# The last projection of a SwiGLU MLP by seven half-size products, with its weight sums made in DRAM

## The chip, the cores and the metric

One core of a Trainium2 chip runs the program. The metric is the time of one execution on the device in microseconds (us), as the median of several executions; lower is better. The engines of the core are TensorE (PE in the profile), VectorE (DVE), ScalarE (ACT), GpSimd (POOL) and SyncE (SP), and 16 DMA engines that all queues share.

## The reference

Two sequences, of 512 and 1024 tokens with 1024 features, go through one layer; everything is float32. With 128 tokens to a tile that is 12 tiles.

```python
D_MODEL = 1024
D_FF = 2816                                     # -(-8 * D_MODEL // (3 * 256)) * 256
def swiglu(hn, w_gate, w_up, w_down):
    return (jax.nn.silu(hn @ w_gate) * (hn @ w_up)) @ w_down
def trunk(x, ...):
    x = x + hybrid_mixer(rmsnorm(x, norm1_g), w_in, ..., w_out)   # dilated attention and gated linear attention
    x = x + swiglu(rmsnorm(x, norm2_g), w_gate, w_up, w_down)
    return rmsnorm(x, final_norm_g)
```

`w_gate` and `w_up` are 1024 x 2816, `w_down` is 2816 x 1024.

## The kernel before

A matrix product in float32 is made of three matmuls of a reduced form: each operand is split into a high part (rounded on ScalarE, L70) and a low part (the remainder, on VectorE, L71), and high x high, high x low and low x high are added in PSUM (`mm3`, L84 to L86). The operations of one engine run in the order in which its queue holds them; a scheduler sets that order from the program's order and the dependencies, and each instruction waits at the head of its queue until its inputs are there.

**The mixer**, 0 to about 920 us, is a list `steps` of some 500 small functions that one loop calls in order: norms of the input rows (`x_a`, `x_b`; their rows come from DRAM by SP's queue at L147), projections, gated linear attention (`Gla`: `e3k_ag` and `e3k_bg` at L607 are multiplied on POOL, the `kv` matmuls at L643 read them), attention, and the output projection. Names that end in `a` or `ag` belong to the first sequence, those in `b` or `bg` to the second. POOL has little to do: among it one power per norm, `rs_n1b` (`rms_rstd`, L65), which VectorE takes to scale the row (L154) before TensorE turns it. Weights and rows come by DMAs on SP's queue, in its order.

**The MLP**, from about 920 us on, works on two blocks of six token tiles; the three pairs of tiles (`NP`) give 3 x 128 = 384 columns (`H`) to each row half. The 2816 features are cut into 11 groups of 256, that is, two halves of 128. Gate and up projections are already made by seven products of half-size matrices (Winograd's form of Strassen's algorithm): `product(wn, n)` is 12 matmuls of 128x384 (L1075) on one combination of weight quarters (`Weights.prepare`, sums on VectorE at L1036, then the split) and one combination of inputs (`b.B[x]`, made once per block by `Block.turn` and kept in DRAM). `common` (L1080) adds the products on VectorE, `w_gate` applies the silu, `w_up` multiplies (L1121) and splits the result into `g`.

The last projection is made in the plain way: `down(i)` (L1129) takes tile i, and for each of two column halves of 512 makes 6 matmuls of 128x512 (two feature halves by three) into a PSUM tile `dn`, which VectorE adds to the running sum `acc` (the tiles `xa`, L1142). The order is a list of units: seven gate products of a group, then the six `down` of the group before, then seven up products. One group thus has 168 gate and up matmuls and 72 down matmuls.

Weights come by `raw` (L1023): 1 MB per group and matrix, `rw_gate`, `rw_up` and `rd` (for `w_down`), each fetched when the one before is used up.

Of the kernel before, what the change touches and what calls it, by code (L numbers as in the profile page):

```python
# [43 lines left out]
def tile_trunk(ctx: ExitStack, tc: tile.TileContext, a: dict):  # L44
# [7 lines left out]
    FORMS = ("b11", "t2", "b21", "t3", "t1", "t4", "b22")  # L52
    formd = {x: [dram.tile([P, 4, 384], F32, name=f"{x}{w}_d") for w in "hl"] for x in FORMS}

# [53 lines left out]
    if True:  # L108
# [758 lines left out]
        for f in steps:  # L867
            f()
        right.close()
# [4 lines left out]
    if True:  # L874
# [5 lines left out]
        g2 = cf.tile([P, D], F32, name="g2")  # L880
# [8 lines left out]
        class Block:  # L889
# [35 lines left out]
            def turn(self, q, tr_p, tag):  # L925
# [21 lines left out]
                sub = lambda o, i0, i1: nc.vector.tensor_tensor(out=o, in0=i0, in1=i1, op=ALU.subtract)  # L947

# [4 lines left out]
                def b11():  # L953
                    tr = quarter(0, 0)
                    sub(t[1], t[3], tr)
                    put("b11", tr)
# [7 lines left out]
                def t1():  # L964
                    put("t1", t[1])
                    sub(t[1], t[2], t[1])

                def b21():
                    put("t2", t[1])
                    tr = quarter(1, 0)  # L970
                    sub(t[1], tr, t[1])
                    put("b21", tr)
# [40 lines left out]
        raws = {}  # L1013

        def raw(blk, grp, wn):

            if wn == "w_down":
                wt = wr_p.tile([P, 2, D], F32, tag="wr", name=f"rd{blk}{grp}")
                src = a[wn][0, grp * 256:(grp + 1) * 256, :].rearrange("(n p) c -> p n c", p=P)
            else:  # L1020
                wt = wr_p.tile([P, KD, 256], F32, tag="wr", name=f"r{wn}{blk}{grp}")
                src = a[wn][0, :, grp * 256:(grp + 1) * 256].rearrange("(k p) c -> p k c", p=P)
            nc.sync.dma_start(out=wt, in_=src)  # L1023
            raws[blk, grp, wn] = wt

        class Weights:


            def __init__(self, blk, grp, wn):
                self.key, self.nm = (blk, grp, wn), f"{wn}{blk}{grp}"  # L1030
                self.w = {}

            def prepare(self, n):
                r = raws[self.key]
                a11, a12, a21, a22 = [r[:, KH * k:KH * k + KH, P * f:P * f + P] for f in range(2) for k in range(2)]
                tt = lambda o, i0, i1, op: nc.vector.tensor_tensor(out=o, in0=i0, in1=i1, op=op)  # L1036
                if n == 1:
                    self.s1, self.s2 = [sm_p.tile([P, KH, P], F32, tag="sm", name=f"{x}{self.nm}") for x in ("s1", "s2")]
# [6 lines left out]
                src = [a11, None, a12, a21, None, a22, a12][n]  # L1045
                src = self.s2 if n == 1 else self.s1 if n == 4 else src
                own, tag = (hx_p, "hx") if n in (2, 5) else (wc_p, "wc")
                wc = own.tile([P, 2, KH, P], F32R, tag=tag, name=f"c{self.nm}{n}")
                split(wc[:, 0], wc[:, 1], src)
                self.w[n] = wc  # L1050
                if n == 6:
                    del raws[self.key]
# [272 lines left out]
```

## Time and profile before

| | us |
|---|---|
| median of 3 executions | 1956.57 |
| lowest, highest | 1955.16, 1958.83 |
| profiled execution | 1959.88 |
| its span, from the first to the last instruction | 1958.1 |
| TensorE busy with matmuls in the span | 1917.9 (98%) |
| VectorE, ScalarE, GpSimd busy | 1377.4 (70%), 849.4 (43%), 80.5 (4%) |
| DMA traffic | 185.16 MB, 95 GB/s over the span |

The profile tells of one execution. Its busy times say how full an engine is, the chain of waits says which work set the end, and the windows give both for a stretch. All rows are times from the span's start; the 1.78 us between span and execution lie before and after it.

### The profile page before, as it was taken

Reading aid. Unit: us, or ns where it says so; the run is one execution under the profiler, and the core shown is the slowest. Engines: PE = TensorE matmul, PEld = TensorE weight load, DVE = VectorE, ACT = ScalarE, POOL = GpSimd, SP = SyncE. Lnnn points to the kernel's source line nnn. Section 1 sums busy time; section 2 is a strip of 40 time slices with the busy share of each in tenths; the row PEclk is TensorE's granted clock in tenths of the full one; section 3 lists DMA queues with packets and bytes.
Section 4 is the critical chain, followed back from the end, with each engine's and each line's share of the span. In section 5 each row is a group of like instructions: output and inputs, shape, how many; then the busy total and the mean of one; then the engine's idle time right before and its main releaser. Section 6 shows DMA issues by size and latency. Waiting matters only on the chain.

```text
span 1958.1 us, 32024 instructions
## 1 busy us (share of the span) xinstructions
PE 1917.9 (98%) x12212; PEld 1769.5 (90%) x12212; DVE 1377.4 (70%) x3158; ACT 849.4 (43%) x2018; POOL 80.5 (4%) x113
## 2 busy tenths in 40 slices
PE   7999999999999999999999999999999999999997
PEld 7888889899998888999999999999998999999997
DVE  5677765737567777554777878797767777777775
ACT  5565555646445455332433434343343333333333
POOL 0110001110000000000000000000020000000001
PEclk9999999999998999999999999999999999999999
DMA  5233230202312233364421425152382222211211
GB/s 141 60 89 90 61 94 20 60 15 59 88 32 77 73 101 96 122 199 139 161 81 65 146 81 162 65 163 85 118 344 86 65 65 78 73 65 65 80 51 65
DMA packets 173642, 185.16 MB, mean 95 GB/s; under 512 B 16752, under 2 KB 149936, under 8 KB 173488
## 3 DMA queue, kind: packets, MB, share of 16 engines
q1 hardware_dynamic: 173488, 183.12, 29.6%
q8 instruction: 96, 1.57, 0.3%
q14 instruction: 58, 0.48, 0.1%
HBM read 151.03 MB, written 32.05 MB: 93 GB/s over the span
## 4 chain that ended last, share of the span: by engine, by line
PE 87%; DVE 4%; DMA 4%; ACT 2%; issue 1%; POOL 1%; SPq 0%; POOLq 0%; DVEq 0%; ACTq 0%
PE gu L1075 32%; PE acc L84 6%; PE acc L86 6%; PE dn L85 6%; PE acc L85 6%; PE dn L86 6%; PE dn L84 6%; PE sc L302 3%; PE pv L402 2%; PE trp L379 2%; PE acco L84 2%; PE acco L85 2%; PE acco L86 2%; PE kv L643 2%; DMA wr_ata<-w_in 1%
## 5 line engine op out<-in xcount | busy, mean ns | idle before, releaser
L1142 DVE TENSOR_TENSOR xa<-dn,xa 128x512 f32<-128x512 f32 x264 | 178.9, 688 | 88.0 <-PE dn L86 86.9
L84 PE MATMUL dn<-wd,g 128*128 128x512 f32 x528 | 205.8, 390 | 2.9 <-ACT wd L70 2.9
L85 PE MATMUL dn<-wd,g 128*128 128x512 f32 x528 | 206.2, 391 | 0.5 <-DVE wd L71 0.5
L86 PE MATMUL dn<-wd,g 128*128 128x512 f32 x528 | 206.0, 390 | 0.0
L70 ACT CAST wd<-rd 128x1024 fp32r<-128x1024 f32 x44 | 44.0, 1047 | 239.6 <-PE dn L86 239.6
L1080 DVE TENSOR_TENSOR u<-gu,u 128x384 f32<-128x384 f32 x176 | 97.3, 553 | 55.0 <-PE gu L1075 54.5
L70 ACT CAST cw_gate<-rw_gate 128x512 fp32r<-128x512 f32 x110 | 67.9, 621 | 125.5 <-PE gu L1075 83.6
L84 PEld LDWEIGHTS dn<-wd,g 128*128 128x128 f32 x528 | 99.2, 188 | 23.0 <-ACT wd L70 3.3
L85 PEld LDWEIGHTS dn<-wd,g 128*128 128x128 f32 x528 | 99.3, 188 | 20.7 <-DVE wd L71 1.2
L86 PEld LDWEIGHTS dn<-wd,g 128*128 128x128 f32 x528 | 99.4, 188 | 20.3
L358 ACT ACTIVATE sm<-sm,st 128x256 f32<-128x256 f32 (+1 forms) x160 | 86.7, 543 | 60.5 <-DVE st L352 60.3
L70 ACT CAST cw_up<-rw_up 128x512 fp32r<-128x512 f32 x110 | 67.7, 620 | 89.7 <-PE gu L1075 43.2
L71 DVE TENSOR_TENSOR cw_up<-rw_up,cw_up 128x512 fp32r<-128x512 f32 x110 | 75.3, 688 | 26.9 <-ACT cw_up L70 25.1
L84 PE MATMUL acc<-w_atb,hnh_b 128*128 128x384 f32 x256 | 91.3, 357 | 0.0
L86 PE MATMUL acc<-w_atb,hnl_b 128*128 128x384 f32 x256 | 88.0, 344 | 0.0
L85 PE MATMUL acc<-w_atb,hnh_b 128*128 128x384 f32 x256 | 87.8, 343 | 0.0
L71 DVE TENSOR_TENSOR cw_gate<-rw_gate,cw_gate 128x512 fp32r<-128x512 f32 x110 | 75.1, 684 | 7.2 <-ACT cw_gate L70 6.8
L379 PE MATMUL trp<-ident,sm 128*128 128x128 f32 x384 | 61.7, 286 | 1.2 <-DVE hnl_b L71 0.7
L347 DVE CUSTOM_DVE_ANT_0 sm<-sc,mask_b 128x256 f32<-128x256 f32 x128 | 49.9, 417 | 17.7 <-PE trqk L254 9.0
L86 PE MATMUL acco<-wo,ml_b 128*128 128x384 f32 (+1 forms) x192 | 61.5, 320 | 0.0
L84 PE MATMUL acco<-wo,mh_b 128*128 128x384 f32 (+1 forms) x192 | 61.3, 319 | 0.0
L85 PE MATMUL acco<-wo,mh_b 128*128 128x384 f32 (+1 forms) x192 | 61.0, 318 | 0.0
(414 smaller groups left out, 5742.0 us busy)
## 6 DMA issues: line engine op xcount, KB each, us to landing
rw_gate<-w_gate SPq DMA_DIRECT2D x22, 1024.0 KB, 5.3
rd<-w_down SPq DMA_DIRECT2D x22, 1024.0 KB, 5.0
rw_up<-w_up SPq DMA_DIRECT2D x22, 1024.0 KB, 5.4
wr_ata<-w_in SPq DMA_DIRECT2D x32, 192.0 KB, 2.5
wr_atb<-w_in SPq DMA_DIRECT2D x32, 192.0 KB, 2.6
wt<-lsed SPq DMA_DIRECT2D x32, 128.0 KB, 3.3
mr_b<-mixd_b SPq DMA_DIRECT2D x8, 512.0 KB, 4.5
xr_b<-x_sample SPq DMA_DIRECT2D x8, 512.0 KB, 4.0
```

Of the source, the lines that this page charges most:

```text
L70: nc.scalar.copy(out=h, in_=src)
L71: nc.vector.tensor_tensor(out=l, in0=src, in1=h.bitcast(F32), op=ALU.subtract)
L84: nc.tensor.matmul(out, xh, wh, start=(k == 0), stop=False)
L85: nc.tensor.matmul(out, xh, wl, start=False, stop=False)
L86: nc.tensor.matmul(out, xl, wh, start=False, stop=(k == n - 1))
L302: nc.tensor.matmul(outs[hd], lhs(x[b:b + 64]), rhs(y[b:b + 64]), start=(n == 0), stop=(n == 2))
L347: nc.vector.tensor_tensor_reduce(out=sm[:, cs], in0=sc[:, cs], in1=mks[g], scale=1.0, scalar=-3e38, op0=ALU.add, op1=ALU.max, accum_out=st ...
L358: nc.scalar.activation(out=sm[:, cs], in_=sm[:, cs], func=AF.Exp, scale=0.125, bias=st[:, NM, pat, hd, i0 + g:i0 + g + 1], accum_out=st[:, ...
L379: nc.tensor.transpose(tr[:, i], sm[:, i * P:(i + 1) * P], ident)
L1075: nc.tensor.matmul(ps, wc[:, wp, k], src[:, k], start=(own == n and k == 0 and i == 0), stop=(k == KH - 1 and i == 2), skip_group_check=True)
L1080: add = lambda o, i0: nc.vector.tensor_tensor(out=o, in0=ps, in1=i0, op=ALU.add)
L1142: nc.vector.tensor_tensor(out=acc[i][:, cs], in0=ps, in1=acc[i][:, cs], op=ALU.add)
```

## The change

**The last projection** is made by seven half-size products too. Two token tiles of a pair are the two row halves, the two feature halves are the inner halves, and the two column halves of `w_down` (512 each) the outer ones. It runs over two groups at a time (`down(blk, grps, n, q)`: product n of pair q, over both groups, 6 matmuls of 128x512); group 10 of each block has no partner and is done as before (`Group.down`, units "e"). The products are chained in PSUM: product 0 starts a fresh sum, 1, 2 and 3 go on in it, 4 starts one, 5 goes on, 6 starts one, and after every product VectorE adds or subtracts the sum into one quarter of `acc`. The left factors are combinations of the four `e` tiles (`left`, split by `factor` into tiles `f_`), the right ones quarters of `w_down` or sums of them. In the order of units each gate product of every second group is followed by the three `down` of the same number, for the two groups before.

**The weight sums** are made once, in DRAM: for each of the three weight matrices four sums of quarters, each in eight row slices. A sum is made by a copy from DRAM to DRAM on SP's queue (L75) and an accumulating DMA on POOL's queue (L80), 360,448 bytes each, 96 of either kind. The sums 2 and 4 add an earlier sum, and so come after its add. The program issues them between the steps of the mixer, from 1/16 to 7/8 of the list.

**The loads** of the MLP: each product's weights come as one quarter or sum, 256 KB each (`fetch`), in place of 1 MB per group and matrix; `prepare` only splits. The weight combinations on VectorE (L1036) are gone. Some signs are turned (`m1`, `m2` for `t1`, `t2`), pool sizes change, and the turn of the second block's inputs starts a group earlier.

```diff
+    FH = FF // 2
+    quarters, sums, bulk = {}, {}, []
+    for wn in ("w_gate", "w_up", "w_down"):
+        w = a[wn][0]
+        if wn == "w_down":
+            q = {(i, j): w[FH * i:FH * i + FH, 512 * j:512 * j + 512] for i in range(2) for j in range(2)}
+            plan = {1: ((0, 0), (0, 1)), 3: ((0, 1), (1, 1)), 2: ((1, 1), 1), 4: ((1, 0), 2)}
+            shape = [FH, 512]
+        else:
+            q = {(i, j): w[512 * j:512 * j + 512, FH * i:FH * i + FH] for i in range(2) for j in range(2)}
+            plan = {1: ((1, 0), (1, 1)), 3: ((0, 0), (1, 0)), 2: ((0, 0), 1), 4: ((0, 1), 2)}
+            shape = [512, FH]
+        quarters[wn] = q
+        sums[wn] = {n: dram.tile(shape, F32, name=f"{wn}s{n}") for n in (1, 2, 3, 4)}
+        step = shape[0] // 8
+        for c in range(8):
+            rows = slice(step * c, step * c + step)
+            def copy(n, wn=wn, plan=plan, rows=rows):
+                nc.sync.dma_start(out=sums[wn][n][rows], in_=quarters[wn][plan[n][0]][rows])
+            def add(n, wn=wn, plan=plan, rows=rows):
+                y = plan[n][1]
+                y = sums[wn][y] if isinstance(y, int) else quarters[wn][y]
+                nc.gpsimd.dma_start(out=sums[wn][n][rows], in_=y[rows], accum_op=ALU.add, max_dma_last_dim=704)
+            bulk.append([(copy, n) for n in (1, 3, 2, 4)])
+            bulk.append([(add, 1), (add, 3)])
+            bulk.append([(add, 2)])
+            bulk.append([(add, 4)])
+    later = [[] for _ in range(len(bulk) // 4 + 3)]
+    for i, x in enumerate(bulk):
+        later[i // 4 + i % 4] += x
+    bulk = [x for y in later for x in y]
...
+        first = len(steps) // 16
+        left_over = list(bulk)
+        for i, f in enumerate(steps):
             f()
+            due = (i - first) * len(bulk) // (len(steps) * 7 // 8 - first)
+            while left_over and len(bulk) - len(left_over) < due:
+                f, n = left_over.pop(0)
+                f(n)
...
-        wr_p = pool(left, "wr", 2, side="left")
-        wc_p = pool(left, "wc", 5, side="left")
-        wd_p = pool(left, "wd", 2, side="left")
-        g_p = pool(left, "g", 1, side="left")
-        e_p = pool(left, "e", 7, side="left")
+        wr_p = pool(left, "wr", 4, side="left")
+        wc_p = pool(left, "wc", 4, side="left")
+        wd_p = pool(left, "wd", 4, side="left")
+        gf_p = pool(left, "gf", 4, side="left")
+        e_p = pool(left, "e", 17, side="left")
         ac_p = pool(left, "ac", 6, side="left")
...
-                    tt(self.s1, a21, a22, ALU.add)
-                    tt(self.s2, self.s1, a11, ALU.subtract)
-                elif n == 3:
-                    tt(a21, a11, a21, ALU.subtract)
-                elif n == 6:
-                    tt(a12, a12, self.s2, ALU.subtract)
...
+        LEFT = ((0, 0), 2, (0, 1), 3, 1, (1, 1), 4)
+        RIGHT = ((0, 0), 2, 3, 4, 1, (1, 1), (1, 0))
...
+            def fetch(self, wn, n):
+                x = (RIGHT if wn == "w_down" else LEFT)[n]
+                src = sums[wn][x] if isinstance(x, int) else quarters[wn][x]
+                lo = self.grp * P
+                nm = f"r{wn}{self.blk}{self.grp}_{n}"
+                own, tag = (sm_p, "sm") if count["raw"] % 2 else (wr_p, "wr")
+                count["raw"] += 1
+                if wn == "w_down":
+                    raw = own.tile([P, 512], F32, tag=tag, name=nm)
+                    nc.sync.dma_start(out=raw, in_=src[lo:lo + P])
+                else:
+                    raw = own.tile([P, KH, P], F32, tag=tag, name=nm)
+                    nc.sync.dma_start(out=raw, in_=src[:, lo:lo + P].rearrange("(k p) c -> p k c", p=P))
+                self.w[wn, n] = raw
+            def prepare(self, wn, n):
+                raw = self.w[wn, n]
+                nm = f"c{wn}{self.blk}{self.grp}_{n}"
+                if wn == "w_down":
+                    wc = wd_p.tile([P, 2, 512], F32R, tag="wd", name=nm)
+                else:
+                    own, tag = (hx_p, "hx") if n in (2, 5) else (wc_p, "wc")
+                    wc = own.tile([P, 2, KH, P], F32R, tag=tag, name=nm)
+                split(wc[:, 0], wc[:, 1], raw)
+                self.w[wn, n] = wc
...
+            def factor(self, nm, src):
+                t = gf_p.tile([P, 2, H], F32R, tag="gf", name=f"{nm}{self.blk}{self.grp}")
+                split(t[:, 0], t[:, 1], src)
+                return t
+            def left(self, n):
+                sub = lambda o, i0, i1: nc.vector.tensor_tensor(out=o, in0=i0, in1=i1, op=ALU.subtract)
+                neg = lambda o, i0, i1: nc.vector.scalar_tensor_tensor(
+                    out=o, in0=i0, scalar=-1.0, in1=i1, op0=ALU.mult, op1=ALU.subtract
+                )
+                a11, a12, a21, a22 = [self.e[x] for x in ((0, 0), (1, 0), (0, 1), (1, 1))]
+                if n == 1:
+                    self.s1, self.s2 = self.tmp("s1"), self.tmp("s2")
+                    sub(self.s1, a22, a21)
+                    neg(self.s2, self.s1, a11)
+                elif n == 2:
+                    sub(a21, a11, a21)
+                elif n == 5:
+                    neg(self.s2, self.s2, a12)
+                src = a11 if n == 0 else self.s2 if n in (1, 5) else (a21, a22, self.s1)[n - 2] if n < 5 else a12
+                self.w["left", n] = self.factor(f"f{n}_", src)
...
+        chain = {}
+        def down(blk, grps, n, q):
+            acc, gs = blocks[blk].acc, [groups[blk, x] for x in grps]
+            fresh = n in (0, 4, 6)
+            if fresh:
+                chain[q] = dn_p.tile([P, 512], F32, tag="dn", name="dn")
+            ps = chain[q]
+            ts = slice(q * P, q * P + P)
+            for i, g in enumerate(gs):
+                x, w = g.w["left", n], g.w["w_down", n]
+                for m, (xp, wp) in enumerate(((0, 0), (0, 1), (1, 0))):
+                    nc.tensor.matmul(ps, x[:, xp, ts], w[:, wp], start=(fresh and i == 0 and m == 0),
+                                     stop=(i + 1 == len(gs) and m == 2), skip_group_check=True)
+            t, c, op = ((0, 0, ALU.add), (0, 1, ALU.subtract), (1, 1, ALU.subtract), (1, 0, ALU.add),
+                        (1, 1, ALU.subtract), (0, 1, ALU.subtract), (0, 0, ALU.add))[n]
+            o = acc[2 * q + t][:, 512 * c:512 * c + 512]
+            nc.vector.tensor_tensor(out=o, in0=o, in1=ps, op=op)
...
-                units += [("p", g, "w_gate", n) for n in range(7)]
-                if prev:
-                    units += [("d", prev, i) for i in range(NT)]
-                units += [("p", g, "w_up", n) for n in range(7)]
...
+                for n in range(7):
+                    units.append(("p", (blk, grp), "w_gate", n))
+                    if prev:
+                        units += [("d", *prev, n, q) for q in range(NP)]
+                units += [("p", (blk, grp), "w_up", n) for n in range(7)]
+                prev = (blk, (grp - 1, grp)) if grp % 2 else None
+            units += [("e", (blk, NG - 1), i) for i in range(NT)]
```

**The order on POOL**, in the mixer's second sequence, around the last norms of its rows and the first `e3k_bg`. Before:

```order
L65 TENSOR_TENSOR rs_n1b_3504<-ms_n1b_3502,nhalf 128x1
L65 TENSOR_TENSOR rs_n1b_3640<-ms_n1b_3638,nhalf 128x1
L65 TENSOR_TENSOR rs_n1b_3772<-ms_n1b_3770,nhalf 128x1
L607 TENSOR_TENSOR e3k_bg_3938<-e3k_bg_3938,qk_bg_3615 128x256
L485 MEMSET st_bg_4048 64x256
```

And now, the same place, where `w_downs` are the sums of quarters of `w_down` in DRAM:

```order
L80 DMA w_downs_84<-w_downs_82 512x176
L80 DMA w_downs_82<-w_downs_81 512x176
L102 TENSOR_TENSOR rs_n1b_3713<-ms_n1b_3711,nhalf 128x1
L80 DMA w_downs_84<-w_downs_82 512x176
L80 DMA w_downs_81<-w_down 176x4x128
L80 DMA w_downs_83<-w_down 176x4x128
L80 DMA w_downs_82<-w_downs_81 512x176
L102 TENSOR_TENSOR rs_n1b_3849<-ms_n1b_3847,nhalf 128x1
L80 DMA w_downs_84<-w_downs_82 512x176
L644 TENSOR_TENSOR e3k_bg_4020<-e3k_bg_4020,qk_bg_3688 128x256
L522 MEMSET st_bg_4133 64x256
L523 MEMSET st_bg_4136 64x256
```

The last of the 96 accumulating DMAs stands directly ahead of the first `e3k_bg`. Ahead of the `rs_n1b` that ran at 232.74 us stand 58 of them, ahead of that of 291.66 us 95.

**The order on SP**, where the rows `x_b` of the second sequence are loaded. Before:

```order
L188 DMA wr_obg_4562<-w_in 128x256
L188 DMA wr_obg_4567<-w_in 128x256
L147 DMA x_b_3480<-x_sample 128x512
L147 DMA x_b_3483<-x_sample 128x512
L147 DMA x_b_3495<-x_sample 128x512
L147 DMA x_b_3498<-x_sample 128x512
```

And now:

```order
L75 DMA w_downs_84<-w_down 176x512
L184 DMA x_b_3550<-x_sample 128x512
L225 DMA wr_obg_4664<-w_in 128x256
L75 DMA w_downs_81<-w_down 176x512
L75 DMA w_downs_83<-w_down 176x512
L184 DMA x_b_3553<-x_sample 128x512
L184 DMA x_b_3565<-x_sample 128x512
L75 DMA w_downs_82<-w_down 176x512
L75 DMA w_downs_84<-w_down 176x512
L75 DMA w_downs_81<-w_down 176x512
L184 DMA x_b_3568<-x_sample 128x512
```

The copies stand between the loads of the rows; with the store of `mixd_a` that ran at 295.98 us all 96 are issued.

**The order on TensorE** in the MLP, after a gate product (`b22h`, `b22l` and the other names of that kind are the high and low parts of input combinations). Before:

```order
L1075 MATMUL gu<-b22l_10637,cw_gate_11824 128x384
L1075 MATMUL gu<-b22h_10636,cw_gate_11824 128x384
L84 MATMUL dn<-wd_11699,g_0_11640 128x512
L85 MATMUL dn<-wd_11699,g_0_11640 128x512
L86 MATMUL dn<-wd_11699,g_0_11640 128x512
L84 MATMUL dn<-wd_11746,g_0_11640 128x512
```

And now:

```order
L1109 MATMUL gu<-b11l_10829,cw_gate_0_12191 128x384
L1109 MATMUL gu<-b11h_10828,cw_gate_0_12191 128x384
L1224 MATMUL dn<-cw_down_0_12270,f_00_12273 128x512 x3
L1224 MATMUL dn<-cw_down_0_12278,f_01_12281 128x512 x3
L1224 MATMUL dn<-cw_down_0_12270,f_00_12273 128x512 x3
L1224 MATMUL dn<-cw_down_0_12278,f_01_12281 128x512 x3
L1224 MATMUL dn<-cw_down_0_12270,f_00_12273 128x512 x3
L1224 MATMUL dn<-cw_down_0_12278,f_01_12281 128x512 x3
L1109 MATMUL gu<-m2h_10830,cw_gate_1_12211 128x384
```

Where 72 down matmuls of one group stood in a row after the seventh gate product, 18 of two groups now stand after each gate product.

## Rows read from the trace of the kernel before

**Rows 1.** The page: busy us of each engine; shares of the chain by engine.

```profile
PE 1917.9 (98%) x12212; PEld 1769.5 (90%) x12212; DVE 1377.4 (70%) x3158; ACT 849.4 (43%) x2018; POOL 80.5 (4%) x113
PE 87%; DVE 4%; DMA 4%; ACT 2%; issue 1%; POOL 1%; SPq 0%; POOLq 0%; DVEq 0%; ACTq 0%
```

**Rows 2.** The chain of waits from 910 us: start us, us, what.

```profile
920.68 5.49 DMA rw_gate<-w_gate
...
991.49 29.23 PE gu L1075 x168
1020.72 0.23 PE dn L84
...
1037.05 29.23 PE gu L1075 x168
```

**Rows 3.** The timeline of TensorE, a down phase: start us, us, instruction.

```profile
1208.05 0.39 PE L84 MATMUL dn<-wd,g 128*128 128x512 f32 x1
...
1209.88 0.39 PE L86 MATMUL dn<-wd,g 128*128 128x512 f32 x1
```

**Rows 4.** Windows: stretch, length, busy us (instructions) by engine, clock, DMA share, GB/s.

```profile
core 0: us, PE busy (x) PEld busy (x) DVE busy (x) ACT busy (x) POOL busy (x), PEclk, DMA share, GB/s
40.00:102.00 62.00, 60.86 (x539) 56.12 (x538) 40.96 (x122) 40.38 (x127) 7.87 (x11) 1.00 0.24 66
102.00:198.00 96.00, 94.38 (x696) 82.50 (x696) 74.93 (x231) 57.46 (x155) 8.82 (x12) 1.00 0.33 88
198.00:233.00 35.00, 34.72 (x239) 28.57 (x238) 23.82 (x73) 19.73 (x49) 1.71 (x4) 1.00 0.29 85
233.00:302.00 69.00, 68.51 (x533) 59.58 (x532) 45.95 (x142) 38.92 (x103) 2.48 (x5) 1.00 0.23 71
...
1506.97:1552.53 45.56, 45.56 (x242) 42.74 (x241) 33.63 (x54) 14.98 (x27) 0.00 (x0) 1.00 0.22 70
...
930.00:935.00 5.00, 5.00 (x30) 5.00 (x30) 4.53 (x7) 4.75 (x7) 0.00 (x0) 1.00 1.03 419
```

**Rows 5.** The page's groups of VectorE: xcount, busy us, mean ns, idle before.

```profile
L1142 DVE TENSOR_TENSOR xa<-dn,xa 128x512 f32<-128x512 f32 x264 | 178.9, 688 | 88.0 <-PE dn L86 86.9
...
L1080 DVE TENSOR_TENSOR u<-gu,u 128x384 f32<-128x384 f32 x176 | 97.3, 553 | 55.0 <-PE gu L1075 54.5
```

**Rows 6.** The timeline of VectorE in the MLP: start us, us, instruction.

```profile
1561.69 0.68 DVE L71 TENSOR_TENSOR cw_gate<-rw_gate,cw_gate 128x512 fp32r<-128x512 f32 x1
1562.29 0.68 DVE L1036 TENSOR_TENSOR s1w_up<-rw_up 128x512 f32<-128x512 f32 x1
...
1564.68 0.55 DVE L1121 TENSOR_TENSOR u<-u,u 128x384 f32<-128x384 f32 x1
1565.15 0.55 DVE L1080 TENSOR_TENSOR c<-gu,u 128x384 f32<-128x384 f32 x1
```

**Rows 7.** The timelines of POOL and of SP's queue in the mixer.

```profile
232.74 0.55 POOL L65 TENSOR_TENSOR rs_n1b<-ms_n1b,nhalf 128x1 f32<-128x1 f32 x1 [13.20 <-DVE rd L364]
...
291.66 0.55 POOL L65 TENSOR_TENSOR rs_n1b<-ms_n1b,nhalf 128x1 f32<-128x1 f32 x1 [8.15 <-DVE ms_n1b L63]
302.08 0.73 POOL L607 TENSOR_TENSOR e3k_bg<-e3k_bg,qk_bg 128x256 f32<-128x256 f32 x1 [9.87 <-ACT e3k_bg L601]
...
264.08 13.38 SPq L147 DMA_DIRECT2D x_b<-x_sample  x6
...
295.98 0.33 SPq L411 DMA_DIRECT2D mixd_a<-oa  x1
```

**Rows 8.** The timeline of VectorE behind one `rs_n1b`.

```profile
292.24 0.88 DVE L154 TENSOR_SCALAR x_b<-x_b,rs_n1b 128x512 f32<-128x512 f32 x2 [0.73 <-POOL rs_n1b L65]
```

**Rows 9.** Line L643 between 300 and 312 us: durations, first and last start.

```profile
L643 PE MATMUL kv<-vt_bg,e3k_bg x8: 272/272/373, 304.9 to 306.4; 64*128 64x128 f32 x8
```

**Rows 10.** DMA issues: count, KB each, median us from issue to landing.

```profile
x_b<-x_sample SPq DMA_DIRECT2D x14, 256.0 KB, 2.7
...
t1l_d<-ft SPq DMA_DIRECT2D x3, 256.0 KB, 5.4
```

More of the change, by code (lines that the diff above doesn't have):

```diff
@@ new lines, in parts, with rows @@
+            def parts(self):
+                self.gt = {x: self.factor(f"g{x[0]}{x[1]}", y) for x, y in self.e.items()}
+            def rows(self, f, c):
+                nm = f"{self.blk}{self.grp}{f}{c}"
+                own, tag = (sm_p, "sm") if count["raw"] % 2 else (wr_p, "wr")
+                count["raw"] += 1
+                raw = own.tile([P, 512], F32, tag=tag, name=f"rd{nm}")
+                nc.sync.dma_start(out=raw, in_=quarters["w_down"][f, c][self.grp * P:self.grp * P + P])
+                self.wd[f, c] = wd_p.tile([P, 2, 512], F32R, tag="wd", name=f"wd{nm}")
+                split(self.wd[f, c][:, 0], self.wd[f, c][:, 1], raw)
@@ new lines, in tile_trunk @@
+                units += [("p", (blk, grp), "w_up", n) for n in range(7)]
+                prev = (blk, (grp - 1, grp)) if grp % 2 else None
+            units += [("e", (blk, NG - 1), i) for i in range(NT)]
+        count = {"raw": 0}
+        blocks.append(Block(1))
+        groups = {(blk, grp): Group(blk, grp) for blk in range(2) for grp in range(NG)}
+        made = [u[1:] for u in units if u[0] == "p"]
+        todo = []
+        ready = 0
+        done = 0
+        for i, u in enumerate(units):
+            if u[0] == "p":
+                while ready < min(done + AHEAD, len(made)):
+                    todo.append((i, *made[ready]))
+                    ready += 1
+                done += 1
+            if u[0] == "d" and u[4] == 0:
+                n = u[3]
+                for m in ((0, 1) if n == 0 else (n + 1,) if n < 6 else ()):
+                    todo += [(i, (u[1], g), "w_down", m) for g in u[2]]
@@ new lines, in tile_trunk, with prepare_to @@
+        fetched = 0
+        def prepare_to(i):
+            nonlocal fetched
+            while todo and todo[0][0] <= i:
+                while fetched < 6 and fetched < len(todo):
+                    _, key, wn, n = todo[fetched]
+                    groups[key].fetch(wn, n)
+                    fetched += 1
+                _, key, wn, n = todo.pop(0)
+                fetched -= 1
+                g = groups[key]
+                g.prepare(wn, n)
+                if wn == "w_down":
+                    g.left(n)
@@ L1230, in tile_trunk @@
         blocks[0].residual()
[L1231 to L1233 removed]
+        TURN = 2
         spare = []
[L1235 removed]
+        for i, u in enumerate(units):
+            prepare_to(i)
             if u[0] == "p":
                 _, key, wn, n = u
[L1238 removed]
                 if key == (1, 0) and wn == "w_gate" and n == 0:
                     blocks[1].residual()
[L1241 to L1246 removed]
+                groups[key].product(wn, n)
```

158 lines of the change are left out of this document (42 added, 116 removed).

## The prediction

> **What bounds the kernel now.** I read the page first, then the chain of waits, then the windows. The page's busy rows put TensorE at 98% of the span, and the chain is 87% PE [rows 1]. So nearly every microsecond of matmul taken away should come back, and nearly every microsecond in which TensorE is starved should be added. The chain's pieces give the MLP's beat [rows 2]: the 168 gate and up matmuls of one group take 29.23 us, the down phase follows from 1020.72 to 1037.05, 16.33 us, and the next group begins. A group is thus 45.56 us, and 16.33 / 72 = 0.227 us is one down matmul, which the starts of single matmuls repeat: (1209.88 - 1208.05) / 8 = 0.229 [rows 3]. In the MLP DMA engines are busy for 22% and VectorE for 33.63 of 45.56 us. In the mixer TensorE is as full: 68.51 of 69 us between 233 and 302 us [rows 4]. Neither stage has idle TensorE time in which a late input could be waited for.
>
> **What it removes.** Per pair of groups, 2 x 72 down matmuls become 7 products x 3 pairs of tiles x 2 groups x 3 = 126; group 10 of each block keeps its 72. Over 2 blocks that is 1584 before and 2 x (5 x 126 + 72) = 1404 after: 180 fewer. They keep the form 128x512, so 180 x 0.2268 = **-40.8 us**, all on the path.
>
> **MLP start.** Before, the first product waits for a 1 MB load, 5.49 us on the chain [rows 2], with the DMA engines full at 419 GB/s between 930 and 935 us [rows 4]. Now quarter tiles of 256 KB come, some of them ahead of the last mixer work. Gain 0 to 5.5; I take **-3**.
>
> **VectorE in the down phase.** The half-size products run inside the gate phase of every second group: per product n, 12 gate matmuls and 18 down matmuls, 12 x 0.174 (29.23 / 168) + 18 x 0.227 = 6.17 us of TensorE. VectorE has in that time six 512-wide operations (three additions into acc, two weight splits, one gate split) and 3.9 of 384 (two splits of factors, 8/7 for combinations, 5/7 for gate sums). By mean durations, 0.688 and 0.553 [rows 5], that is 6.26 us, over the budget; but operations behind each other start 0.60 and 0.47 apart (1561.69 to 1562.29; 1564.68 to 1565.15) [rows 6], so they fill 5.4, 88%. The chained products in PSUM make the next product's matmul wait only for its own weights, not for the addition. The 176 weight combinations at L1036 are gone. DMA carries 42 x 256 KB per 87 us, about 126 GB/s, against 70 in the window of a group [rows 4], in a stage that did 419. I take **+5** for waits here, block ends included, bounds 0 and +20: at the upper one VectorE's 6.26 governs the 70 products, 6, and each block's end with its six late splits of e and four of w_down costs 7.
>
> **The bulk DMAs, on which the sign hangs.** 96 copies from DRAM to DRAM on SP's queue and 96 accumulating DMAs on POOL's queue, 360 KB each, are written to be spread over the mixer. The order shows otherwise. On SP the copies stand among the loads of x_b, from 264 us, and all 96 ahead of the store of mixd_a at 295.98; all 96 adds stand on POOL ahead of the instruction that made e3k_bg at 302.08 [rows 7], 58 of them ahead of rs_n1b of 232.74. Both queues are in order. Each add waits for its copy or an earlier add, so POOL's small operations queue behind all earlier ones. Who waits for those: VectorE's x_b at 292.24 idled 0.73 us for rs_n1b [rows 8]; kv's matmuls start at 304.9, 2 us after e3k_bg was done [rows 9]. So there is about 2 us of slack, and then TensorE stands.
>
> The budget is 302 - 40 = 262 us for 96 pairs, 2.73 us each, less what the mixer itself moves: its DMA share between 40 and 233 is 0.29 (0.24, 0.33, 0.29), leaving 0.71; between 233 and 302 it is 0.23, leaving 0.77 [rows 4]. The price of a pair stands in no row, since no row shows DRAM to DRAM or an accumulation. The nearest is the MLP's start, full at 419 GB/s [rows 4]. The lower bound takes 360,448 bytes once at that rate: 0.86 us for a copy and the same for an add. For the add I take 1.72 us, since it reads two operands where a load reads one; the upper bound counts every byte read and written, 1.72 for a copy and 2.58 for an add.
> - At the middle, 0.86 + 1.72 = 2.58 a pair: 58 x 2.58 / 0.71 = 211 us in the first 193, so 18 late; 38 x 2.58 / 0.77 = 127 in 69, so 58 late. With 2 of slack taken off, about **+75**.
> - At the lower, 1.72 a pair: the first stretch holds (141 of 193), the second takes 85 of 69: +16, or nothing if the mixer's loads give way.
> - At the upper, 4.30 a pair: 158 + 143 = +301; with a dear copy and the middle add, 3.44 a pair, 88 + 101 = +189.
>
> The middle is nearest to the rows of plain loads, with only the second operand added. POOL's side of it: of the four adds of a step two depend on each other, so at the 2.7 to 5.4 us from issue to landing of 256 KB [rows 10] 24 steps take 130 to 259 us of 262. That alone would just fit.
>
> The Trainium skill speaks against the cheap end: "DMA: Bandwidth & Descriptors", section "Latency and other measured facts", gives 207 to 214 GB/s per direction for copies between HBM tensors. As an estimate from that page a copy is 1.7 us, and the sum by it would be that of the case with 3.44 a pair. No run here shows it yet.
>
> **Sum.** Against the profiled execution of 1959.88 (its span is 1958.1): 1959.88 - 40.8 - 3 + 5 + 75 = 1996. The median is 3.3 lower than that execution, so **1993** for the median. Without lag it would be 1918.
>
> **Rivals.**
> - *The adds are hidden or cheap* (faster). A pair costs 1.72 us, because a DMA engine's reading and writing overlap and nothing but the source counts. Lag 0 to 35, centre 16: 1918 + 16 = 1934, from 1915 to 1950. For it: the mixer's DMA engines are idle for 70% and more [rows 4]. Against it: 1.72 x 38 = 65 us must still pass in the 69 us in which TensorE has no gap. It decides below 2.2 us a pair.
> - *Both directions count, or POOL's chain does* (slower by far). 3.44 a pair gives 1918 + 189 = 2107; 4.30 gives 2219. For it: the adds come in rows of 704 bytes and go through another queue than all loads before, of which no row shows anything; the landings above fit only if they stay under 5.4 us. Against it: loads from and stores to DRAM mix in the mixer's rows without a slower landing (2.7 us) [rows 10]. The mechanism: late adds hold POOL, POOL holds rs_n1b and e3k_bg, these hold TensorE. (The rule of the Trainium skill named above would act here in this way.)
> - *Within 0.2%*: lag and gain cancel (lag 35 to 43). That is a point between two cases and no mechanism.
> - *The MLP loses what it gains*: the new stage runs at VectorE's pace or its loads come late. It would need 41 us over 10 pairs, 4 us each, where I see at most 0.6. I give it no chance of its own; it is in the +20.
>
> **How the numbers follow.** Forecast (lag 47 to 112: 1965 to 2030) 0.36; the cheap rival 0.31; the dear rival 0.27; within 0.2% 0.06. 0.2%, 4 us, is about what a measurement of this kernel can tell from no change. Faster 0.31, same 0.06, slower 0.36 + 0.27 = 0.63. The likeliest case's own range is 1965 to 2030; since cases of both signs hold most of the chance, the range for 8 in 10 reaches to 1920 (half of the cheap rival's lower part left out, some 5 in 100) and to 2180 (the dear rival beyond 3.9 us a pair left out, some 12 in 100).
>
> **What the changed profile would show.** Down matmuls of L1224 and the last groups at 1404 in all and 0.227 us apart; pairs of groups at 87.0 us rather than 91.1; MLP from first gate product to end about 41 us shorter: step one. TensorE idle between 200 and 400 us of the old clock, released by POOL's rs_n1b or e3k_bg, with DMA near 100% in that stretch and POOL's queue waiting for DMA: the lag. If DMA is near 100% and TensorE not idle, the adds were cheap and the mixer's loads gave way. If POOL waits while the DMA engines are half idle, it was the chain of landings or the making of descriptors, not bandwidth, and the price per pair is a latency. If the mixer ends at 920 as before, the forecast is wrong at its second term. If the MLP's pair is over 88 us with TensorE released by DVE, the third term was too small.

## The result, and the profile after

The changed kernel takes 2087.02 us (2081.72 to 2088.55) against 1957.7: the ratio is 1.0653, 95% interval 1.0624 to 1.0681. It is slower, as forecast, but by 129 us where 36 were forecast. Its profiled execution is 2081.72 us, its span 2079.9, 121.8 more than before.

The page of the changed kernel: busy us of the engines, the chain by engine, DMA share and GB/s in 40 slices, and the two DMA queues (packets, MB, share).

```profile
PE 1925.7 (93%) x12032; PEld 1766.4 (85%) x12032; DVE 1358.9 (65%) x3196; ACT 916.3 (44%) x2182; POOL 189.8 (9%) x209
...
DMA  7999999951111222324665374755458434434441
GB/s 193 203 221 228 236 238 249 205 69 42 42 48 52 59 82 66 104 86 138 196 208 149 117 213 122 218 158 171 136 208 304 142 113 146 130 108 137 116 144 66
...
q1 hardware_dynamic: 316944, 268.08, 42.2%
q0 software_dynamic: 53760, 34.61, 12.9%
...
PE 71%; DMA 11%; issue 7%; DVE 4%; POOL 3%; ACT 2%; SPq 1%; POOLq 0%; DVEq 0%; ACTq 0%
```

The matmuls are 180 fewer, as they should be, yet PE's share of the chain falls from 87% [rows 1] to 71%. The second row shows where: the DMA engines are full from the second slice to the eighth, and move 200 to 250 GB/s meanwhile, where the MLP's start before moved 419 at the same share [rows 4].

Three rows of POOL and one of VectorE at the place of [rows 7, 8] (the timelines of the changed kernel):

```profile
362.08 1.01 POOL L80 DMA_DIRECT2D w_downs<-w_downs  x1 [15.28 <-DMA w_downs<-w_downs]
...
378.30 1.66 POOL L102 TENSOR_TENSOR rs_n1b<-ms_n1b,nhalf 128x1 f32<-128x1 f32 x1
...
449.16 0.72 POOL L644 TENSOR_TENSOR e3k_bg<-e3k_bg,qk_bg 128x256 f32<-128x256 f32 x1 [6.15 <-ACT e3k_bg L638]
...
379.99 1.13 DVE L191 TENSOR_SCALAR x_b<-x_b,rs_n1b 128x512 f32<-128x512 f32 x2 [32.66 <-POOL rs_n1b L102]
```

The add at 362.08 has waited 15 us at the head of POOL's queue for an earlier one to land. Behind it and more adds of the same kind comes the power at 378.30, and VectorE stands 32.66 us for it; before, no such wait was longer than 0.73 us. The first `e3k_bg` runs at 449.16 instead of 302.08, 147 us late. The waits from 24 us to there give it in one row (waiting engine, what released it: us in total, times, longest):

```profile
DVE x_b L191 <- POOL rs_n1b L102: 80.0, 8, 32.7
...
POOL w_downs L80 <- DMA w_downs<-w_downs: 53.3, 7, 15.3
...
POOL w_ups L80 <- DMA w_ups<-w_up: 47.9, 11, 8.4
```

Before, the first of these was 4.0 us in 6 times. In all POOL's queue waits 234 us of these 425 for copies and adds to land. The windows of the same work, from 24 us to the first `e3k_bg`, of the kernel before and of the changed one (columns as in [rows 4]):

```profile
24.00:302.00 278.00, 271.81 (x2092) 239.84 (x2092) 190.82 (x578) 162.58 (x450) 21.43 (x31) 0.99 0.28 80
```

```profile
24.00:449.00 425.00, 315.98 (x2099) 273.55 (x2097) 194.16 (x578) 162.55 (x451) 132.51 (x127) 0.82 1.04 215
```

TensorE's idle time rises from 6 to 109 us. The other 44 us of the 147 are matmuls that take longer: the same 2,100 take 316 us instead of 272, at a granted clock of 0.82 instead of 0.99. Share times length gives the DMA engines' work: 278 x 0.28 = 78 us before, 425 x 1.04 = 442 now, so 364 / 96 = **3.8 us for a pair** of copy and add. (The share adds up the time of all packets, so it can pass 1; these prices are time of all 16 engines, not the length of one transfer.)

The MLP, from the first gate product to the end, takes 1031.2 us before (1958.1 - 926.9) and 1008.0 now (2079.9 - 1071.9), 23 less. The chain of the changed kernel in the second block:

```profile
1690.03 45.92 PE gu L1109 x264
...
1777.08 45.92 PE gu L1109 x264
...
1864.13 45.92 PE gu L1109 x264
...
1951.18 45.92 PE gu L1109 x264
```

Every pair of groups is 87.05 us here, against 91.12 before [rows 2], and TensorE waits for nothing. (In the first block three pairs take longer; the account of the waits in the MLP, below, has them.)

### The profile page after: what moved, and what is told of

Its sections match the earlier page's. It is cut to its first block, busy times and chain, and to the rows that moved or that the text cites. A ratio compares the mean times of both kernels' runs of the same rounds, so it can differ in the third digit from the quotient of the medians.

```text
span 2079.9 us, 33335 instructions
## 1 busy us (share of the span) xinstructions
PE 1925.7 (93%) x12032; PEld 1766.4 (85%) x12032; DVE 1358.9 (65%) x3196; ACT 916.3 (44%) x2182; POOL 189.8 (9%) x209
## 3 DMA queue, kind: packets, MB, share of 16 engines
q0 software_dynamic: 53760, 34.61, 12.9%
## 4 chain that ended last, share of the span: by engine, by line
PE 71%; DMA 11%; issue 7%; DVE 4%; POOL 3%; ACT 2%; SPq 1%; POOLq 0%; DVEq 0%; ACTq 0%
PE gu L1109 27%; PE dn L1224 14%; PE acc L121 5%; PE acc L123 4%; PE acc L122 4%; PE sc L339 3%; PE acco L121 2%; PE acco L122 2%; PE acco L123 2%; DMA w_ups<-w_ups 2%; PE trp L416 2%; PE pv L439 2%; DMA w_downs<-w_down 1%; PE kv L680 1%; POOL w_downs L80 1%
## 5 line engine op out<-in xcount | busy, mean ns | idle before, releaser
L1224 PE MATMUL dn<-cw_down,f 128*128 128x512 f32 x1260 | 298.9, 390 | 0.1
L1224 PEld LDWEIGHTS dn<-cw_down,f 128*128 128x128 f32 x1260 | 235.2, 188 | 46.1 <-DVE cw_down L108 0.9
L107 ACT CAST cw_gate<-rw_gate 128x512 fp32r<-128x512 f32 x154 | 95.3, 621 | 180.5 <-PE gu L1109 105.3
L1229 DVE TENSOR_TENSOR xa<-xa,dn 128x512 f32<-128x512 f32 x210 | 143.3, 687 | 22.9 <-PE dn L1224 21.5
L107 ACT CAST cw_up<-rw_up 128x512 fp32r<-128x512 f32 x154 | 95.1, 619 | 112.5 <-PE gu L1109 91.4
L108 DVE TENSOR_TENSOR cw_up<-rw_up,cw_up 128x512 fp32r<-128x512 f32 x154 | 106.0, 691 | 55.5 <-ACT cw_up L107 51.5
L108 DVE TENSOR_TENSOR cw_gate<-rw_gate,cw_gate 128x512 fp32r<-128x512 f32 x154 | 105.8, 690 | 46.9 <-ACT cw_gate L107 37.4
L107 ACT CAST cw_down<-rw_down 128x512 fp32r<-128x512 f32 x140 | 85.8, 619 | 88.1 <-PE dn L1224 73.1
L108 DVE TENSOR_TENSOR cw_down<-rw_down,cw_down 128x512 fp32r<-128x512 f32 x140 | 96.1, 690 | 15.3 <-ACT cw_down L107 12.8
L416 PEld LDWEIGHTS trp<-ident,sm 128*128 128x128 f32 x384 | 49.1, 155 | 47.5 <-DVE hnl_b L108 30.5
```

What stands on the lines that cost most here:

```text
L107: nc.scalar.copy(out=h, in_=src)
L108: nc.vector.tensor_tensor(out=l, in0=src, in1=h.bitcast(F32), op=ALU.subtract)
L416: nc.tensor.transpose(tr[:, i], sm[:, i * P:(i + 1) * P], ident)
L1224: nc.tensor.matmul(ps, x[:, xp, ts], w[:, wp], start=(fresh and i == 0 and m == 0), stop=(i + 1 == len(gs) and m == 2), skip_group_check=True)
L1229: nc.vector.tensor_tensor(out=o, in0=o, in1=ps, op=op)
```

## The experiments

The lag of a kernel is its time less that of the kernel without bulk DMAs, 1933.7. Rows with one execution are marked with a star; where there are four, their lowest and highest lie 3 to 15 us apart, so differences of a few us between rows tell nothing.

| kernel | us | lag |
|---|---|---|
| no bulk DMAs | 1933.67 | 0 |
| copies only * | 1949.09 | 15 |
| copies and plain transfers in place of the adds * | 2001.65 | 68 |
| changed kernel | 2087.02 | 153 |
| changed, adds in long rows * | 2056.92 | 123 |
| changed, POOL's small operations moved away * | 1995.2 | 62 |
| a third of the pairs * | 1999.47 | 66 |
| two thirds of the pairs * | 2009.17 | 75 |
| all pairs, spread | 1985.11 | 51 |

**Without the bulk DMAs.** The edit: `left_over = []`, and `fetch` reads quarter (0, 0) for a sum.

> The changed kernel without the 96 copies and 96 accumulating DMAs; the loads that would read a sum read the quarter (0, 0) in its place, so the products of the sums are computed on other numbers. Theory (the lag is all the bulk DMAs' doing): the first e3k_bg on POOL is back near 302 us instead of 449, the first gate product near 922 instead of 1072, and the time is 2087 - 150 = 1937, between 1930 and 1945, that is faster than the kernel before by 1%. Rival (a part of the 150 us comes from the other edits, the pools or the order): 1960 or more.

1933.67 us (1930.1 to 1935.12), ratio to before 0.9873, interval 0.9859 to 0.9888, as the theory says. The rest of the change gains 24 us, and the whole loss is the bulk DMAs'.

**What a copy and an add cost.** First `def add(...): return`; then the add without its accumulation; then the accumulation with longer rows:

```diff
-nc.gpsimd.dma_start(..., in_=y[rows], accum_op=ALU.add, max_dma_last_dim=704)
+nc.gpsimd.dma_start(..., in_=y[rows], max_dma_last_dim=704)
```
```diff
-nc.gpsimd.dma_start(..., in_=y[rows], accum_op=ALU.add, max_dma_last_dim=704)
+nc.gpsimd.dma_start(..., in_=y[rows], accum_op=ALU.add, max_dma_last_dim=5632)
```

> The 96 copies remain, the 96 accumulating DMAs are left out, so each sum is only its first quarter. Busy share times length of the DMA engines from 24 to 442 us is 438 us in the changed kernel against 79 in the same work of the kernel before (24 to 302 us), so 3.7 us for a pair of copy and add. Theory A (bytes count in both directions, and an accumulation reads a second operand): a copy takes about 1.5 us of all DMA engines, 144 in all, the share between 24 and 302 us rises to about 0.8, and since 144 + 79 is less than 278 the mixer is not late: 1937 to 1950. Rival B (a copy is as dear as an add, 1.85): 178 + 79 = 257 of 278, share 0.92, 1940 to 1965.

> The 96 DMAs on POOL's queue stay with their shapes, their rows of 704 bytes, their waits and their order, but copy instead of accumulating, so each sum is its last operand. Theory A (the accumulation's second read makes it dear): a DMA on POOL's queue falls to the price of a copy, the pair from 3.7 to about 3.0 us, and the lag of the first e3k_bg from 147 to about 80: 2015. Rival B (rows of 704 bytes and the other queue make it dear, or the chain of waits does): price and lag stay, 2075 to 2090.

> The changed kernel with the adds' rows cut at 5632 bytes instead of 704 (64x1408 and 176x512 elements), all else the same. Without accumulating, a DMA of the 704-byte form cost 213/96 - 107/96 = 1.10 us of the DMA engines, with it 363/96 - 1.12 = 2.66, and the accumulating queue sent 53,760 packets against 10,752. Theory A (the small rows make the accumulation dear): packets fall to some 11,000, an add to 1.1 to 1.6 us, the lag of the first e3k_bg from 147 to 50 to 85 us: 1990 to 2020. Rival B (the second operand read from DRAM and the read and write of the destination make it dear, byte by byte): an add stays at 2.4 to 2.7 us, lag 125 to 147: 2060 to 2090.

Windows from 24 us to the first `e3k_bg`, of copies only, of plain transfers, of long rows:

```profile
24.00:315.00 291.00, 278.19 (x2105) 242.90 (x2104) 191.99 (x580) 162.75 (x454) 21.17 (x32) 0.98 0.64 195
```

```profile
24.00:367.00 343.00, 289.52 (x2100) 250.55 (x2099) 192.36 (x579) 162.28 (x452) 88.73 (x128) 0.92 0.85 267
```

```profile
24.00:418.00 394.00, 303.64 (x2096) 263.88 (x2095) 193.20 (x579) 161.92 (x450) 99.45 (x127) 0.87 0.94 232
```

Less 79 us for the mixer's own, divided by 96: a copy is (186 - 79) / 96 = **1.1 us**, copy and plain transfer (292 - 79) / 96 = 2.2, so the plain transfer on POOL's queue 1.1 too, and an add 3.8 - 1.1 = **2.7 us**, 2.4 times the same bytes without accumulation. The profile's row of POOL's queue (packets, MB, share of the span) says the same without a difference; of the changed kernel, of the spread order below, of plain transfers, of long rows:

```profile
q0 software_dynamic: 53760, 34.61, 12.9%
```

```profile
q0 software_dynamic: 53760, 34.61, 13.6%
```

```profile
q0 software_dynamic: 10752, 34.61, 5.6%
```

```profile
q0 software_dynamic: 9472, 34.61, 9.6%
```

Share times span divided by 96 is 2.8, 2.8, 1.2 and 2.1 us. In the spread order the engines are not full (a share of 0.68), so the price is not an effect of full engines. With rows of 5632 bytes the packets on POOL's queue fall from 53,760 to 9,472 and the add to (370 - 79) / 96 - 1.1 = 1.9 us. Both causes are real: row length is worth 0.8 us of an add, the accumulation itself, at nearly the same number of packets, another 0.8. (Both expectations of the last run lay beside it: 2056.92 is just below the rival's range.) The copies alone cost 15 us without full DMA engines (0.64). The loads of `x_b`, queued among them on SP, land in 6.1 us at the median instead of 2.7, and ScalarE waits 15.9 us for them instead of 10.7; that this is the whole of the 15 isn't shown.

**Who carries the lag.** `nc.gpsimd` becomes `nc.vector` for `e3k` and the settings to zero, and a constant made on VectorE stands for the powers, so that POOL issues adds only:

> The changed kernel with POOL's small operations of the mixer moved to VectorE: the product e3k, the settings to zero, and the norms' power, which is left out (a constant stands for it, so the norms are wrong). POOL issues nothing but the adds; copies and adds stand where they stood. Theory A (the DMA engines themselves are too full and the mixer's own loads come late): the lag of the first e3k_bg stays at 110 to 147 us: 2050 to 2085. Rival B (late adds hold POOL and so rs_n1b and e3k_bg): without them the mixer waits only for its loads, as with the copies alone or the spread order, 15 to 60 us: 1950 to 1995.

1995.2 us, at the edge of rival B. The DMA engines are as full (a share of 1.07 from 24 to 369 us), but the lag is 62 instead of 153. So, by this one execution, some 90 us come from adds that hold POOL's queue. The other 60 are put down to transfers that make the mixer's own loads late: in this run ScalarE waits 39.3 us in 12 times for `x_b`, against 10.7 before.

**Fewer pairs.** `if wn not in ("w_down",): continue` ahead of the bulk, or the other two matrices:

> Only the sums of w_down are made, 32 copies and 32 adds; where a sum of w_gate or w_up would be read, a quarter is. Theory A (work against room: a pair costs 3.78 us, the mixer's own transfers 79, and 278 us lie between 24 and 302): 32 x 3.78 + 79 = 200 fits, lag 0 to 15: 1934 to 1950. Rival B (each add costs its chain of landings on POOL, wherever): the lag is in proportion, 147 / 3 = 49: 1975 to 1990.

> Only the sums of w_gate and w_up are made, 64 copies and 64 adds; w_down's are read from a quarter. Theory A: 64 x 3.78 + 79 = 321 against 278, lag 43 to 60 with the loads' own delay: 1977 to 1995. Rival B (in proportion): 147 x 2 / 3 = 98: 2025 to 2040.

1999.47 and 2009.17: 66 us for a third and 75 for two thirds fit neither theory. The windows of the run with a third show why:

```profile
60.00:100.00 40.00, 21.87 (x131) 19.91 (x130) 13.16 (x40) 13.01 (x38) 15.38 (x15) 0.63 1.22 259
100.00:150.00 50.00, 30.95 (x170) 26.58 (x171) 14.48 (x45) 10.20 (x35) 22.20 (x20) 0.60 1.17 184
150.00:200.00 50.00, 48.84 (x439) 45.03 (x439) 32.26 (x95) 32.13 (x92) 8.26 (x11) 1.00 0.31 73
```

All 32 adds were put among POOL's first products (`e3k_ag`) and norms (`rs_ag`) and run between 38 and 150 us; behind them TensorE waits 25.9 us in 4 times for `e3k_ag`, and VectorE 24.8 us in 7 times for `rs_ag`. TensorE is busy for 53 of the 90 us from 60 to 150, at a granted clock of 0.6. The room up to 302 us doesn't count; what stands ahead of a small operation in its queue does. In the run with two thirds VectorE waits 18.5 us for `rs_n1b` and ScalarE 26.6 us for `wr_ata` (9.0 before); how its 75 us divide isn't worked out.

**Spread.** Each copy and add is held behind the last instruction that its queue had in the program's order:

```diff
+eng = mybir.EngineType.SP if f.__name__ == "copy" else mybir.EngineType.Pool
+with tc.issue_after(next(x for x in reversed(nc.cur_bb.bb.instructions) if x.engine == eng)):
     f(n)
```

> The changed kernel, complete, with each copy queued behind the SP instruction and each add behind the POOL instruction that stood last in the program's order, so that they are spread over the mixer as written (the last 29 adds stand behind POOL's last operation of the mixer). Theory A (the DMA engines' work of 3.7 us a pair is what came too densely): 96 x 3.7 = 358 us over 880 us with a share of 0.27 of the mixer's own gives a share of about 0.68, the lag goes to 0 to 25 us, and the time is 1937 to 1962. Rival B (POOL's queue is held by each add's wait for landings wherever it stands): every add still delays the small operations behind it, a lag of 50 to 150: 1990 to 2087.

1985.11 us (1982.44 to 1988.95), ratio 1.0141, between the two theories: two thirds of the lag are gone, and 51 us remain. No wait for POOL of over 1.1 us is left. What the profile shows in its place is loads: ScalarE's waits for `wr_ata` and `wr_atb` in the mixer rise from 9.0 and 6.1 us to 22.2 and 24.0, and so does the median landing of these weights (of before, and of the spread kernel; columns as in [rows 10]):

```profile
wr_ata<-w_in SPq DMA_DIRECT2D x32, 192.0 KB, 2.5
wr_atb<-w_in SPq DMA_DIRECT2D x32, 192.0 KB, 2.6
```

```profile
wr_ata<-w_in SPq DMA_DIRECT2D x32, 192.0 KB, 4.9
wr_atb<-w_in SPq DMA_DIRECT2D x32, 192.0 KB, 6.3
```

Three tries to remove that failed. Long rows in the spread order, then the copies on ScalarE's queue (`nc.scalar.dma_start`), then the turn of block 1's inputs back to its old place (`TURN = 3`, rows in the gate phase, turn in the up phase):

> The spread order of the run before (1985) with rows of 5632 bytes. Theory A (price of an add by its rows): the DMA engines' share in the mixer falls from 0.67 to about 0.5, the 51 us of lag to 20 to 35: 1955 to 1970. Rival B (price by bytes): 1980 to 1990.

> The same, and the copies are issued on ScalarE's queue instead of SP's. In the spread order the mixer's weight loads (192 KB) took 4.9 and 6.3 us to land against 2.5 and 2.6 before. Theory A (they queue behind the copies on SP's own queue): their landing falls to 2.5 to 3.5 us and at least half of the lag that is left goes: 10 to 20 us less than the run with copies on SP. Rival B (the DMA engines are shared, whichever queue): landing and time within 5 us of that run.

> The same as the run with copies on ScalarE's queue, and the turning of the second block's inputs back where it was before the change: rows fetched in the gate phase, turned in the up phase of groups 3, 5 and 7. In the changed kernel a pair of groups with a turn takes 92.7 to 93.4 us and one without 87.05; before a turn cost 1.95. Theory: each of the three turns costs 2 instead of 5.6 to 6.3 us: 10 to 13 us less than the run without this. Rival (the turn's work on VectorE or its stores are what is late, wherever it stands): within 4 us of it.

1998.06, 2011.89 and 2001.51 us. Long rows make the spread order 13 us slower, beyond both theories, though the adds are cheaper and the DMA engines less full (a share of 0.57 from 24 to 900 us, against 0.68); why is open. On ScalarE's queue the weights land in 2.9 and 2.8 us, as theory A says, yet the time is 14 us longer: a shorter median landing isn't the lag. ScalarE's wait for `wr_atb` stayed as it was, 22.7 us in 10 times, against 22.7 in 8. So what the spread order still loses is open. The third is 10 us less than the second, but all of it ahead of the MLP (988.3 against 1005.9 in the profiled executions), which the edit doesn't touch, and no more than the executions of one kernel differ; the MLP takes 1009.6 us against 1008.4, and a turn costs 6.0 to 7.4 us. For the MLP the rival holds.

**Buffers of the MLP.** On the kernel without bulk DMAs, `wc` 4 to 5 and `e` 17 to 15:

> The kernel without the bulk DMAs (1933.7; sums replaced by a quarter) with five buffers wc instead of four and 15 buffers e instead of 17. The turning of the second block's inputs takes its tiles fm, fb, ft from wc, as the split weights do, and frees them only when their stores have landed. Theory (the buffer wc that the change took away is what makes a turn cost 5.6 to 6.7 us against 1.95 before): three turns and the start of block 1 get back 8 to 14 us: 1920 to 1926. Rival (VectorE's fuller row of work, or the loads, makes the turns dear): within 3 us, 1931 to 1937, or slower where 15 buffers e are too few.

1921.93 us, 12 less, within the theory's range, but not from the turns, which still cost 6 to 7.4 us each (5.6 to 7.8 without the edit). From the up phase of group 10 to that of block 1's group 1 it is 78.3 us instead of 92.0, with 74.8 of matmuls: the start of block 1 had lost 17 us and loses 3.5.

**Less in DRAM.** With five `wc`: the sums of `w_gate` and `w_up` made on POOL in the MLP, in place in the loaded quarters, and only those of `w_down` in DRAM, spread (two choices of buffers); then these too moved into the MLP's first block but for two groups, with spaced and with dense turns.

```diff
+                add = lambda o, i0, i1: nc.gpsimd.tensor_tensor(out=o, in0=i0, in1=i1, op=ALU.add)
...
+                    t10 = self.quarter(wn, 1, 0)
+                    t11 = self.quarter(wn, 1, 1)
+                    self.w[wn, 3] = s3 = self.raw(wn, "s3")
+                    add(s3, self.w[wn, "q00"], t10)
+                    add(t10, t10, t11)
```

> Complete. Only w_down's sums are made in DRAM: 32 copies and 32 adds, spread over the mixer as in the spread run. The sums of w_gate's and w_up's quarters are made in the MLP on POOL, which is idle there, in place in the loaded quarters, four additions of 128x512 a matrix; each matrix then takes four loads instead of seven. Five buffers wc, 13 e, 5 wr. Without bulk DMAs and with five wc the time was 1921.9. Theory A (the lag follows the amount, 51 us for 96 spread pairs): 17 for 32, so 1939, between 1930 and 1955, faster than before by 1%. Rival B (accumulation as such costs some 50 us in the mixer): 1965 to 1985. Rival C (POOL's additions come too late for the second product, some 5 us a matrix): each group over 43.5 us, 44 x 2 to 5 us more.

> The same with 15 buffers e and 4 wr instead of 13 and 5. Theory (raw quarters, held longer now, need the fifth wr more than the group needs e): slower than the run with 13 and 5 by 2 to 15 us. Rival (13 buffers e are too few): faster by as much.

> Complete. As the run with sums of w_gate and w_up on POOL (1981.9), but the sums of w_down are made by group, 8 copies and 8 adds of 256 KB in the mixer's second half for the first two groups, the other 32 and 32 during the MLP's first block, each some 30 products ahead of its use; group 10 needs none. The pieces of a turn are given after every second product instead of every one. Theory A (transfers hurt where loads are on the path, in the mixer; the MLP's loads are far enough ahead): the lag goes from 29.6 to 3 to 8 us, and with turns at 6 to 10 us instead of 14 the time is 1981.9 - 24 - 12 to 24 = 1934 to 1946. Rival B (the MLP is as sensitive): steady pairs of groups in the first block over 88 us and the time within 10 us of 1982, or above.

> The same with the turn's pieces after every product, as in the changed kernel. Theory A: 12 to 24 us more than the run with spaced pieces, 1950 to 1962. Rival (the turn's cost lies in its tiles and stores, not in how densely its pieces come): within 4 us of it.

1981.87, 1987.03, 1994.72 and 1993.44 us. The first two can't be told apart (ratios 1.0099 to 1.0129 and 1.0104 to 1.0155), nor can the last two. In the first the MLP starts 28 us later than in the run with five `wc` and no bulk DMAs (951.2 against 922.9), where 17 were expected, and block 0's turns cost 14 us each instead of 6 to 7; why is open. Without a turn POOL's sums cost nothing:

```profile
1590.74 46.00 PE gu L1149 x264
...
1677.87 45.96 PE gu L1149 x264
...
1764.96 46.03 PE gu L1149 x264
```

In the third and fourth the lag of the mixer is nearly gone (first gate product at 929.2 and 927.2 us), but the first block pays it back, in the pairs of groups beside which the adds run: in the third a pair with a turn takes 109 us instead of 101 in the first, the pair ahead of them 97 instead of 87, and the last, beside which there are no adds, 87.06. POOL's sums queue behind adds, and ScalarE waits longer for POOL (between 1000 and 1400 us 19.1 us for `rw_up` and 33.1 for `rw_gate`, 12.9 and 17.6 in the first); that these waits are the whole of it isn't shown. The pacing of the turns made no difference, as the rival of the last run says. No version here that computes the whole is faster than the kernel before.

## Why the prediction was wrong

- **180 matmuls, -40.8 us.** Right: 4.07 us a pair of groups, 10 pairs, -40.7.
- **MLP start, -3.** Right in kind, too small: TensorE waits 0.6 us ahead of the first product instead of 3.4, the first group's gate phase takes 14.7 us instead of 18.0, and the next phase gives 0.8 more, some -7 in all. Of the 3.3 us of the gate phase 1.7 are a wait for split weights at its end; the rest are matmuls that took longer, since from 926.92 to 930 us, behind the wait, the granted clock was 0.50, that is, 1.2 GHz, where it is 1.00 now.
- **Waits in the MLP, +5, bounds 0 and +20.** Too small: +21. Not VectorE's pace, which I had put behind the bound: the pairs without a turn show no wait. A pair with a turn costs 5.6 to 6.4 us more than one without, where it was 1.95 (3 turns, +12.5), and the start of block 1 loses 16.5 us instead of 8.5 (+8). I had taken the turns as unchanged and had not counted that the edit gave `wc` one buffer less. A fifth buffer (with two fewer `e`) regains the block's start. What the turns wait for is open; in the chain they go through a load of rows and through stores that free `wc` buffers:

```profile
1173.75 12.55 PE gu L1109 x72
...
1186.32 3.71 DMA hx<-x2d_b
...
1192.11 1.30 DVE hx L959
...
1205.20 3.96 DMA m1l_d<-fm
...
1209.91 0.69 DVE fm L108
```

- **The bulk DMAs, +75.** The step that failed, in three places. The price: I took 0.86 for a copy and 1.72 for an add, nearest to plain loads; they are 1.1 and 2.7. My upper bound, bytes counted both ways, was 2.58 for the add: the true price lay above it, since 704-byte rows cost 0.8 of it. The form: I divided the bulk's time by the free share of the DMA engines, as if the mixer's own transfers grew with the delay; their 79 us are fixed. Taken so, 96 x 2.58 + 79 - 278 = 49, and with 3.8 it is 166 where 147 was measured. The two errors went against each other: the right price in the old form would have given +234. And POOL's chain, which I let "just fit": the adds land in 6.3 to 9.2 us at the median where I had taken 2.7 to 5.4, and my 24 steps of two landings then take 302 to 442 us instead of 130 to 259. The path I had named, late adds that hold POOL and with it `rs_n1b` and `e3k_bg`, is the one that the run with POOL freed shows, for 90 of 153 us. Whether full DMA engines or the long landings set the pace of the adds isn't told apart: both sums come near the 425 us. The landings were not short in the spread order either (6.0 to 9.5 us, at a share of 0.68).
- **The dear rival**, 3.44 a pair and 2107 us at 0.27, was nearer than the forecast; the cheap one fell. I let the cheap one decide below 2.2 us a pair; that was the price with plain transfers, and even that costs 68 us.
- The Trainium skill, "DMA: Bandwidth & Descriptors", section "Latency and other measured facts", gives 207 to 214 GB/s per direction for copies of 128 rows of 16 KiB between HBM tensors, and lower rates for some distances between the rows. Here a copy of 360,448 bytes takes 1.1 us of the DMA engines, some 320 GB/s, where the estimate from the page was 1.7 us. The measurement decides for these copies, and not the copy made the pair dear but the add.
- **TensorE's clock** wasn't in the sum: 44 of the 147 us are matmuls that take longer, at a granted clock of 0.82 instead of 0.99.

## What to carry to other kernels

Ask of every asynchronous transfer which small operation stands behind it in the same queue: the scheduler here put all 96 adds ahead of an operation on which everything waits. Price work in DRAM by a run of its own before a design rests on it; an accumulation is not a copy with one more read. Where TensorE was at 98%, a microsecond of waiting cost 1.4 here (147 of lag for 103 of idle time), since the matmuls beside it ran at a lower clock.

## What had not been expected of the hardware

- An accumulating DMA from DRAM to DRAM takes 2.4 times the DMA engines' time of the same transfer without accumulation (2.7 against 1.1 us for 352 KB), and sends five times the packets in rows of 704 bytes (53,760 against 10,752).
- Landing in DRAM, issue to end: 6.3 to 9.2 us for such an add, 4.9 to 7.2 for the plain transfer.
- POOL adds 128x512 in 1.3 to 1.5 us at the median beside a VectorE busy for 68.43 of 87.13 us (one pair of groups of that run), and no pair of groups without a turn was longer for it by more than 0.12 us.
- A shorter landing of the loads (2.8 and 2.9 us instead of 5.1 and 6.2, by another queue for the copies) made the kernel no faster.
